# Weight blocks of a seven-product matrix multiplication: two sums made by an accumulating transfer, paired splits, and 15 instead of 12 of 22 tiles

## The chip, the cores and the metric

One core of one Trainium2 chip runs the whole program. The metric is the device time of one execution in microseconds, as the median of several runs. Engines are named as in the profile: PE (TensorE matmuls), PEld (its weight loads), DVE (VectorE), ACT (ScalarE), POOL (GpSimd), SP (SyncE, which here issues transfers).

## What is computed

Two layers, each of a feed-forward block, a mixer (an attention of several branches in the first layer, a latent attention "MLA" in the second) and a second feed-forward block, on 512 tokens of width 1024, all in 32-bit floats:

```
def _swiglu(x, w_gate, w_up, w_down):
    return (jax.nn.silu(x @ w_gate) * (x @ w_up)) @ w_down
...
for l in range(DEPTH):
    x = x + 0.5 * _swiglu(_rms_norm(x, ffn1_norm[l]), ffn1_w_gate[l], ffn1_w_up[l], ffn1_w_down[l])
    h = _rms_norm(x, mix_norm[l])
    ...
    x = x + 0.5 * _swiglu(_rms_norm(x, ffn2_norm[l]), ffn2_w_gate[l], ffn2_w_up[l], ffn2_w_down[l])
return _rms_norm(x, final_norm)
```

The feed-forward width is 2816, that is 22 tiles of 128. The change concerns the products with `w_gate` and `w_up` in the four feed-forward blocks.

## The kernel before, in words

The stages run in the order f0, e, f1, f2, m, f3: four feed-forward blocks (FFN) around the mixers e and m. Activations lie transposed, features on partitions and the 512 tokens along the free axis, as eight tiles of 128x512.

Every factor is split into a high part, rounded to the float32r format on ACT, and the remainder, made on DVE. A product is then three matmuls (`mm3`, lines 208 to 210): high by high, high by low, low by high.

An FFN (`ffn`) does its 22 tiles in two halves of 11, each followed by the down projection of that half. An ordinary tile takes the weights of gate and up, 128x1024 each; each product is 8 x 3 matmuls of 512 columns, 48 in all. A tile listed in `SEVEN` (line 32) treats gate and up together as a 2x2 block product: the two halves of the features by the two halves of the tokens. Seven products of half size (`seven`, lines 301 to 343) take the place of eight: 7 x 4 x 3 = 84 matmuls of 256 columns. Their left factors are four blocks of the weights and four sums: A11, A12, A22, r21 (which is only a summand), S1 = r21 + r22, S2 = S1 + A11, S3 = A11 + r21, S4 = A12 + S2. The right factors are halves of x and the tiles T12 and T34 that `combine` makes once in an FFN. Before the change the pattern of the tiles from 4 on is two with seven products, then one ordinary.

`fetch_seven` (line 164) makes the left factors: two loads of 512 KB on SP's queue (lines 170 and 171), four adds on DVE (line 174), and for each of seven blocks a copy on ACT (line 180) and a subtraction on DVE (line 181). They lie two by two in tiles `wh` and `wl`: (A11, S2), (S1, S3), (A12, S4), and A22 alone in `w3h` and `w3l`. For other weights `fetch` (line 144) loads 512 KB (line 154) and splits it in one piece of 1024 columns (lines 160 and 161).

What sets the order is a list of the weights in the order of use (`plan`) and `chunk`, which keeps two entries fetched ahead. Within that, a scheduler places each engine's instructions in one in-order queue; buffers (three each of `w`, `wh` and `wl`) decide how far a load or a split can really run ahead. On an engine's queue, whatever stands behind a waiting instruction waits with it.

Other lines that are spoken of: in `norm`, ACT and DVE split x (lines 217 and 218), `squares` adds squares on POOL (line 231), `rstd` sums them on PE (line 241) into `rv` (line 246, DVE) and takes the power on POOL (`rcol`, line 251), and `spread` turns that into the row `rrow` by four transposes on PE (line 260). The evacuation of a tile multiplies by this row.

Of the kernel before, what the change touches and what calls it, by code (L numbers as in the profile page):

```python
# [3 lines left out]
P = 128  # L4
D, SEQ, FF = 1024, 512, 2816
# [3 lines left out]
F32, F32R = mybir.dt.float32, mybir.dt.float32r  # L9
AF, OP, AX = mybir.ActivationFunctionType, mybir.AluOpType, mybir.AxisListType  # L10
# [14 lines left out]
def raw(ap):  # L25
    return ap.bitcast(F32)
# [2 lines left out]

SEVEN = (4, 5, 7, 8, 10, 11, 13, 14, 16, 17, 19, 20)

FFNS = {"f0": ("f1", 0, 0), "f1": ("f2", 0, 2), "f2": ("f1", 1, 3), "f3": ("f2", 1, 5)}

# [42 lines left out]
class Core:  # L78
# [47 lines left out]
    def plan(self, stages):  # L126

        todo = []
        for st in stages:
            if st in FFNS:  # L130
                name, l, _ = FFNS[st]
                for h in range(2):
                    for f in range(h * HF, h * HF + HF):
                        if f in SEVEN:
                            todo.append(("seven", name, l, f))
# [28 lines left out]
    def fetch_seven(self, name, l, f):  # L164

        nc, kp, sb = self.nc, self.keep, self.sb
        g, u = [kp.tile([P, 1024], F32, name="w", bufs=3) for _ in range(2)]
        nc.sync.dma_start(g, self.a[name + "_g"][l, f])  # L170
        nc.sync.dma_start(u, self.a[name + "_u"][l, f])
        a11, a12, r21, r22 = g[:, :SEQ], g[:, SEQ:], u[:, :SEQ], u[:, SEQ:]
        s1, s2, s3, s4 = [sb.tile([P, SEQ], F32, name=f"s{i}") for i in range(1, 5)]
        add = lambda o, a, b: nc.vector.tensor_tensor(o, a, b, OP.add)
        out = {}

        def parts(blocks, h, l):
            for i, (n, src) in enumerate(blocks):
                c = slice(i * SEQ, i * SEQ + SEQ)
                nc.scalar.activation(h[:, c], src, AF.Copy)  # L180
                nc.vector.tensor_tensor(l[:, c], src, raw(h[:, c]), OP.subtract)
                out[n] = h[:, c], l[:, c]

        def pair():
            return [kp.tile([P, 1024], F32R, name=n, bufs=3) for n in ("wh", "wl")]
        add(s1, r21, r22)
        add(s2, s1, a11)
        parts((("A11", a11), ("S2", s2)), *pair())
        add(s3, a11, r21)
        parts((("S1", s1), ("S3", s3)), *pair())  # L190
        add(s4, a12, s2)
        parts((("A12", a12), ("S4", s4)), *pair())
        parts((("A22", r22),), *[sb.tile([P, SEQ], F32R, name=n) for n in ("w3h", "w3l")])
        return out

    def chunk(self, *key):
# [148 lines left out]
    def ffn(self, name, l, gi, then=None):  # L345

        nc = self.nc
        with self.tc.tile_pool(name="ff", bufs=1, reuse_waits="tile") as sb:
# [3 lines left out]
            for half in range(2):  # L352
                ah, al = [], []
                for i in range(HF):
                    f = half * HF + i
                    a = sb.tile([P, SEQ], F32, name="fa", bufs=2)
                    if f in SEVEN:
                        g, n = self.seven(sb, ("seven", name, l, f), xs, T, R)
# [574 lines left out]
def constants(np):  # L933

    c = {"ident": np.eye(P, dtype=np.float32)}
    p = np.arange(P)[:, None]
    j = np.arange(SEQ)[None, :]
    d = p + 384 - j
    big = np.float32(BIG)
    c["mcau"] = np.where(d >= 0, np.float32(0), big).astype(np.float32)  # L940
    n = ((d >= 0) & (d <= 128)).astype(int) + ((d >= 0) & (d % 4 == 0)) + ((d >= 0) & (d % 16 == 0))
    c["mdil"] = np.where(n > 0, -np.log(np.maximum(n, 1).astype(np.float64)), BIG).astype(np.float32)
    t = np.arange(P)[:, None, None] + P * np.arange(4)[None, :, None]
    e = (16 * np.arange(32) + 31)[None, None, :]
    ok = (e <= t)
    c["mcmp"] = np.stack([np.where(ok, np.float32(0), big), ok.astype(np.float32)], axis=1).astype(np.float32)

    def table(dims):
        inv = np.float32(500000.0) ** (-np.arange(0, dims, 2, dtype=np.float32) / np.float32(dims))
        ang = np.arange(SEQ, dtype=np.float32)[:, None] * inv[None, :]  # L950
        return np.cos(ang).T, np.sin(ang).T
    co, si = table(16)
    cp, sp = np.ones((P, SEQ), np.float32), np.zeros((P, SEQ), np.float32)
    for b in (0, 64):
        cp[b:b + 8], cp[b + 8:b + 16] = co, co
        sp[b:b + 8], sp[b + 8:b + 16] = -si, si
    c["cos_p"], c["sin_p"] = cp, sp
    co, si = table(32)
    sc = np.float32(-(96.0 ** -0.5))
    one, c2, s2 = np.ones((64, SEQ), np.float32), np.concatenate([co, co]), np.concatenate([-si, si])  # L960
    c["cs_q"] = np.stack([np.concatenate([one, c2, s2]), np.concatenate([c2, s2, one])]) * sc
    c["cs_k"] = np.stack([np.tile(c2, (4, 1)), np.tile(s2, (4, 1))], axis=1)
    return {k: np.ascontiguousarray(v, dtype=np.float32) for k, v in c.items()}


def layout(np, i):

    i = {k: np.asarray(v) for k, v in i.items()}
    d = {"x": i["x"][0].T}
    d["g"] = np.concatenate(  # L970
        [v.reshape(-1, P).T for v in (i["ffn1_norm"][0], i["mix_norm"][0], i["ffn2_norm"][0], i["ffn1_norm"][1],
                                      i["mix_norm"][1], i["ffn2_norm"][1], i["final_norm"],
                                      i["mla_q_norm"][0], i["mla_kv_norm"][0])]
        + [np.zeros((P, 1), np.float32)], axis=1)
    for n in ("1", "2"):
        for s, t in (("gate", "g"), ("up", "u")):
            w = i[f"ffn{n}_w_{s}"]
            d[f"f{n}_{t}"] = w.reshape(2, KT, P, NF, P).transpose(0, 3, 2, 1, 4).reshape(2, NF, P, 1024)
        w = i[f"ffn{n}_w_down"].reshape(2, 2, HF, P, KT, P).transpose(0, 1, 4, 2, 3, 5)
        d[f"f{n}_d"] = w.reshape(2, 2, HF, 8, P, P).transpose(0, 1, 2, 4, 3, 5).reshape(2, 2, HF, P, 1024)  # L980

    def feat(w):

        k, n = w.shape[0] // P, w.shape[1] // P
        return w.reshape(k, P, n, P).transpose(2, 1, 0, 3).reshape(n, P, k * P)

    def out_parts(w, parts):

        w = w.reshape(8, P, KT, P)
        res = []  # L990
        for pairs in parts:
            n = len(pairs)
            v = w[list(pairs)].transpose(2, 0, 1, 3).reshape(n, 8, P, P)
            res.append(v.transpose(0, 2, 1, 3).reshape(n, P, 1024))
        return np.concatenate(res)

    def tok(w, n):

        w = w.reshape(KT, P, -1)
        pad = -KT % n  # L1000
        if pad:
            w = np.concatenate([w, np.zeros((pad,) + w.shape[1:], w.dtype)])
        return w.reshape(-1, n, P, w.shape[2]).transpose(0, 2, 1, 3).reshape(len(w) // n, P, -1)
    w = i["ev_w_in"][0]
    cols = [w[:, c:c + n] for c, n in ((C_QA, 512), (C_KC, 128), (C_VC, 128), (C_KS, 128), (C_KW, 128),
                                       (C_QB, 512), (C_KB, 512))]
    d["ev_in"] = feat(np.concatenate(cols, axis=1))
    d["ev_vsw"] = tok(np.concatenate([w[:, C_VS:C_VS + 128], w[:, C_VW:C_VW + 128], w[:, C_G:C_G + 24]], axis=1), 3)
    d["ev_vb"] = np.stack([tok(w[:, C_VB + 256 * j:C_VB + 256 * j + 256], 4) for j in range(2)])
    d["ev_out"] = out_parts(i["ev_w_out"][0], EV_PARTS)  # L1010
    w = np.stack([i[f"nsa_cmp_pos_{s}"][0].reshape(16, 2, 64).transpose(2, 1, 0) for s in "kv"], axis=1)
    d["pos"] = np.concatenate([w, w])
    d["cmp_w1"] = np.stack([i[f"nsa_cmp_{s}_w1"][0].reshape(2, 8, P, P).transpose(0, 2, 1, 3).reshape(2, P, 1024)
                            for s in "kv"])
    d["cmp_w2"] = np.stack([np.concatenate([i[f"nsa_cmp_{s}_w2"][0]] * 2, axis=1) for s in "kv"], axis=1)
    w = i["mla_w_in"][0]
    d["mla_in"] = feat(np.concatenate([w[:, :384]] + [w[:, 384:416]] * 4, axis=1))
    w = i["mla_w_uq"][0].reshape(2, P, 16, 96)
    n, r, z = w[..., :64], w[..., 64:], np.concatenate([w[..., 80:], w[..., 64:80]], axis=-1)
    w = np.stack([np.concatenate([n, r, z], axis=-1)[:, :, 0::2], np.concatenate([r, z, n], axis=-1)[:, :, 1::2]],  # L1020
                 axis=3)
    d["mla_uq"] = w.reshape(2, P, 4, 4, P).transpose(2, 1, 3, 0, 4).reshape(4, P, 1024)
    w = i["mla_w_ukv"][0].reshape(P, 2, 8, 2, 64).transpose(1, 0, 3, 2, 4)
    d["mla_ukv"] = w.reshape(2, P, 1024)
    d["mla_out"] = out_parts(i["mla_w_out"][0], ML_PARTS)
    d.update(constants(np))
    return {k: np.ascontiguousarray(v) for k, v in d.items()}
# [18 lines left out]
```

## Time and profile before

| | us |
|---|---|
| median of 3 runs | 1916.21 (1915.01 to 1916.22) |
| the profiled execution | 1913.86 |
| its span, first to last instruction | 1911.7 |
| PE busy | 1883.0 (98%) |
| DVE busy | 1354.5 (71%) |
| ACT busy | 903.4 (47%) |
| POOL busy | 274.6 (14%) |
| mean share of the DMA engines | 0.30, at 91 GB/s |

Matmuls overlap in the profile (each lasts longer than the distance to the next), so what a matmul costs is read from the distance between starts. The rows of the timeline give start, duration, engine, line, operation, result and operands, shape, and how many equal ones were merged; the windows give busy time by engine in a stretch of the span.

### The profile page before, as it was taken

Reading aid. Unit: us, or ns where it says so; the run is one execution under the profiler, and the core shown is the slowest. Engines: PE = TensorE matmul, PEld = TensorE weight load, DVE = VectorE, ACT = ScalarE, POOL = GpSimd, SP = SyncE. Lnnn points to the kernel's source line nnn. Section 1 sums busy time; section 2 is a strip of 40 time slices with the busy share of each in tenths; the row PEclk is TensorE's granted clock in tenths of the full one; section 3 lists DMA queues with packets and bytes.
Section 4 is the critical chain, followed back from the end, with each engine's and each line's share of the span. In section 5 each row is a group of like instructions: output and inputs, shape, how many; then the busy total and the mean of one; then the engine's idle time right before and its main releaser. Section 6 shows DMA issues by size and latency. Waiting matters only on the chain. (4 is left out here: it accounts for less than half of the span.)

```text
span 1911.7 us, 27981 instructions
## 1 busy us (share of the span) xinstructions
PE 1883.0 (98%) x10850; PEld 1657.4 (87%) x10850; DVE 1354.5 (71%) x2438; ACT 903.4 (47%) x1585; POOL 274.6 (14%) x291
## 2 busy tenths in 40 slices
PE   9999999999999999999999999999999999999998
PEld 6998998878887789889988988998878879989987
DVE  8764875477888888468756864885489888747853
ACT  7432443347586654234435432443378664424432
POOL 0000000274454400000010000000156320000001
PEclk9999999999999999999999999999999999999999
DMA  4232333323111123323333232333311122333231
GB/s 170 86 113 87 110 98 109 118 89 93 58 45 34 45 85 114 100 89 109 111 92 96 82 118 89 100 108 102 123 39 33 56 89 89 111 99 100 89 110 67
DMA packets 49846, 174.67 MB, mean 91 GB/s; under 512 B 5793, under 2 KB 6049, under 8 KB 49713
## 3 DMA queue, kind: packets, MB, share of 16 engines
q1 hardware_dynamic: 48960, 171.74, 29.1%
q8 instruction: 85, 1.39, 0.3%
q10 hardware_dynamic: 720, 1.08, 0.2%
q14 instruction: 49, 0.39, 0.1%
q0 software_dynamic: 32, 0.07, 0.0%
HBM read 170.76 MB, written 2.10 MB: 90 GB/s over the span
## 5 line engine op out<-in xcount | busy, mean ns | idle before, releaser
L160 ACT ACTIVATE wh<-w 128x1024 fp32r<-128x1024 f32 (+1 forms) x217 | 229.2, 1057 | 357.7 <-PE pt L209 98.3
L161 DVE TENSOR_TENSOR wl<-w,wh 128x1024 fp32r<-128x1024 f32 (+1 forms) x217 | 273.0, 1259 | 159.4 <-ACT wh L160 158.3
L208 PE MATMUL pa<-xh,wh 128*128 128x512 f32 (+1 forms) x736 | 269.1, 366 | 2.8 <-ACT wh L160 2.2
L210 PE MATMUL pa<-xh,wl 128*128 128x512 f32 (+1 forms) x736 | 268.2, 364 | 0.5 <-DVE wl L161 0.5
L209 PE MATMUL pa<-xl,wh 128*128 128x512 f32 (+1 forms) x736 | 268.7, 365 | 0.0
L231 POOL TENSOR_TENSOR of<-of,t 128x512 f32<-128x512 f32 x36 | 55.9, 1552 | 1319.6 <-issue 892.5
L209 PE MATMUL pb<-xl,wh 128*128 128x256 f32 (+1 forms) x704 | 233.9, 332 | 0.2
L208 PE MATMUL pb<-xh,wh 128*128 128x256 f32 (+1 forms) x704 | 233.6, 332 | 0.0
L210 PE MATMUL pb<-xh,wl 128*128 128x256 f32 (+1 forms) x704 | 233.3, 331 | 0.0
L180 ACT ACTIVATE wh<-w 128x512 fp32r<-128x512 f32 x96 | 60.7, 632 | 237.9 <-PE pb L209 159.2
L208 PEld LDWEIGHTS pa<-xh,wh 128*128 128x128 f32 x736 | 139.9, 190 | 26.0 <-ACT wh L160 3.5
L210 PEld LDWEIGHTS pa<-xh,wl 128*128 128x128 f32 x736 | 139.7, 190 | 22.1 <-DVE wl L161 1.0
L209 PEld LDWEIGHTS pa<-xl,wh 128*128 128x128 f32 x736 | 139.9, 190 | 20.8 <-DVE xl L218 0.4
L209 PEld LDWEIGHTS pb<-xl,wh 128*128 128x128 f32 x704 | 133.8, 190 | 15.0 <-DVE xl L218 2.6
L208 PEld LDWEIGHTS pb<-xh,wh 128*128 128x128 f32 x704 | 133.8, 190 | 12.9 <-ACT xh L217 0.4
L210 PEld LDWEIGHTS pb<-xh,wl 128*128 128x128 f32 x704 | 133.8, 190 | 12.3
L180 ACT ACTIVATE wh<-s 128x512 fp32r<-128x512 f32 x192 | 114.9, 622 | 55.9 <-PE pa L209 26.3
L208 PE MATMUL pc<-fah,wh 128*128 128x512 f32 x352 | 137.0, 389 | 0.0
L209 PE MATMUL pc<-fal,wh 128*128 128x512 f32 x352 | 137.0, 389 | 0.0
L210 PE MATMUL pt<-fah,wl 128*128 128x512 f32 x352 | 136.9, 389 | 0.0
L210 PE MATMUL pc<-fah,wl 128*128 128x512 f32 x352 | 136.9, 389 | 0.0
L208 PE MATMUL pt<-fah,wh 128*128 128x512 f32 x352 | 136.9, 389 | 0.0
(264 smaller groups left out, 4556.3 us busy)
## 6 DMA issues: line engine op xcount, KB each, us to landing
w<-f_g SPq DMA_DIRECT2D x88, 512.0 KB, 3.7
w<-f_u SPq DMA_DIRECT2D x88, 512.0 KB, 3.6
w<-f_d SPq DMA_DIRECT2D x88, 512.0 KB, 3.7
w<-ev_in SPq DMA_DIRECT2D x16, 512.0 KB, 3.7
w<-ev_out SPq DMA_DIRECT2D x8, 512.0 KB, 3.3
w<-mla_out SPq DMA_DIRECT2D x8, 512.0 KB, 3.3
x<-x SPq DMA_DIRECT2D x8, 256.0 KB, 5.3
w<-ev_vb SPq DMA_DIRECT2D x4, 512.0 KB, 3.2
```

The source lines that it names most:

```text
L160: nc.scalar.activation(h[:, :cols], w[:, :cols], AF.Copy)
L161: nc.vector.tensor_tensor(l[:, :cols], w[:, :cols], raw(h[:, :cols]), OP.subtract)
L180: nc.scalar.activation(h[:, c], src, AF.Copy)
L208: nc.tensor.matmul(out, wh, xh, start=start, stop=False)
L209: nc.tensor.matmul(out, wh, xl, start=False, stop=False)
L210: nc.tensor.matmul(out, wl, xh, start=False, stop=stop)
L231: eng.tensor_tensor(parts[0], parts[0], sq, OP.add)
```

## The change

`SEVEN` lists 15 tiles: from tile 4 on four with seven products follow each other, then one is ordinary (shorter at the end of a half: 9 and 10, 11 and 12, 19 to 21). The host lays the four blocks of such a tile out side by side as A12, r22, A11, r21 in one array `f1_s` or `f2_s`. S1 and S3 are no longer added on DVE: SP loads r21 twice side by side into a new tile `s13` (two buffers), and when it has landed POOL issues a transfer of r22 and A11, side by side, that adds to what lies there. A11 and A12 are loaded into the first halves of two `w` tiles, whose second halves take S2 and S4 from DVE. So each pair lies in one tile, and is split by one ACT copy and one DVE subtraction of 1024 columns. r22 has a tile of its own, with one buffer.

```
-SEVEN = (4, 5, 7, 8, 10, 11, 13, 14, 16, 17, 19, 20)
+SEVEN = (4, 5, 6, 7, 9, 10, 11, 12, 14, 15, 16, 17, 19, 20, 21)
...
-        g, u = [kp.tile([P, 1024], F32, name="w", bufs=3) for _ in range(2)]
-        nc.sync.dma_start(g, self.a[name + "_g"][l, f])
-        nc.sync.dma_start(u, self.a[name + "_u"][l, f])
-        a11, a12, r21, r22 = g[:, :SEQ], g[:, SEQ:], u[:, :SEQ], u[:, SEQ:]
-        s1, s2, s3, s4 = [sb.tile([P, SEQ], F32, name=f"s{i}") for i in range(1, 5)]
-        add = lambda o, a, b: nc.vector.tensor_tensor(o, a, b, OP.add)
+        src = self.a[name + "_s"][l, SEVEN.index(f)]
+        u1, u3 = [kp.tile([P, 1024], F32, name="w", bufs=3) for _ in range(2)]
+        u2 = sb.tile([P, 1024], F32, name="s13", bufs=2)
+        r22 = sb.tile([P, SEQ], F32, name="r22")
+        nc.sync.dma_start(u2.rearrange("p (a b) -> p a b", a=2),
+                          src[:, 3 * SEQ:].unsqueeze(1).to_broadcast([P, 2, SEQ]))
+        nc.gpsimd.dma_start(u2, src[:, SEQ:3 * SEQ], accum_op=OP.add)
+        nc.sync.dma_start(u1[:, :SEQ], src[:, 2 * SEQ:3 * SEQ])
+        nc.sync.dma_start(u3[:, :SEQ], src[:, :SEQ])
+        nc.sync.dma_start(r22, src[:, SEQ:2 * SEQ])
         out = {}
 
-        def parts(blocks, h, l):
-            for i, (n, src) in enumerate(blocks):
+        def parts(names, t, h, l):
+            nc.scalar.activation(h, t, AF.Copy)
+            nc.vector.tensor_tensor(l, t, raw(h), OP.subtract)
+            for i, n in enumerate(names):
                 c = slice(i * SEQ, i * SEQ + SEQ)
-                nc.scalar.activation(h[:, c], src, AF.Copy)
-                nc.vector.tensor_tensor(l[:, c], src, raw(h[:, c]), OP.subtract)
                 out[n] = h[:, c], l[:, c]
...
-        add(s1, r21, r22)
-        add(s2, s1, a11)
-        parts((("A11", a11), ("S2", s2)), *pair())
-        add(s3, a11, r21)
-        parts((("S1", s1), ("S3", s3)), *pair())
-        add(s4, a12, s2)
-        parts((("A12", a12), ("S4", s4)), *pair())
-        parts((("A22", r22),), *[sb.tile([P, SEQ], F32R, name=n) for n in ("w3h", "w3l")])
+        nc.vector.tensor_tensor(u1[:, SEQ:], u2[:, :SEQ], u1[:, :SEQ], OP.add)
+        parts(("A11", "S2"), u1, *pair())
+        parts(("S1", "S3"), u2, *pair())
+        nc.vector.tensor_tensor(u3[:, SEQ:], u3[:, :SEQ], u1[:, SEQ:], OP.add)
+        parts(("A12", "S4"), u3, *pair())
+        parts(("A22",), r22, *[sb.tile([P, SEQ], F32R, name=n) for n in ("w3h", "w3l")])
```

The first place is DVE's queue in the second half of f0, where the left factors of a seven-product tile are made between the evacuations of earlier tiles (numbers are buffer numbers). Before, for tile 14:

```order
L174 TENSOR_TENSOR s1_1938<-w_1935 128x512
L174 TENSOR_TENSOR s3_1940<-w_1934,w_1935 128x512
L174 TENSOR_TENSOR s2_1939<-s1_1938,w_1934 128x512
L373 TENSOR_TENSOR fa_1874<-pb_1968,fg_1993 128x512
L181 TENSOR_TENSOR wl_1900<-w_1875,wh_1899 128x512
L181 TENSOR_TENSOR wl_1900<-s4_1882,wh_1899 128x512
L377 TENSOR_TENSOR fal_1998<-fa_1874,fah_1997 128x512
L174 TENSOR_TENSOR s4_1941<-w_1934,s2_1939 128x512
L181 TENSOR_TENSOR wl_1945<-w_1934,wh_1944 128x512
L181 TENSOR_TENSOR wl_1945<-s2_1939,wh_1944 128x512
L330 TENSOR_TENSOR fv_2013<-fm_2014,pa_2008 128x256
L181 TENSOR_TENSOR wl_1952<-s1_1938,wh_1951 128x512
```

And now, around tiles 14 to 16 (`s13_2030`, `s13_2082` and `s13_2143` are the pairs S1, S3 of these three tiles; line 190 is the S2 add, 193 the S4 add, 183 the split):

```order
L183 TENSOR_TENSOR wl_2043<-s13_2030,wh_2042 128x1024
L379 TENSOR_TENSOR fal_2024<-fa_1915,fah_2023 128x512
L375 TENSOR_TENSOR fa_2027<-pb_2107,fg_2132 128x512
L183 TENSOR_TENSOR wl_2048<-w_2029,wh_2047 128x1024
L379 TENSOR_TENSOR fal_2137<-fa_2027,fah_2136 128x512
L190 TENSOR_TENSOR w_2141<-s13_2143,w_2141 128x512
L183 TENSOR_TENSOR wl_2091<-w_2080,wh_2090 128x1024
L332 TENSOR_TENSOR fv_2173<-fm_2174,pa_2168 128x256
L183 TENSOR_TENSOR wl_2095<-s13_2082,wh_2094 128x1024
L335 TENSOR_TENSOR fm_2174<-fv_2173,pt_2170 128x512
L193 TENSOR_TENSOR w_2142<-w_2142,w_2141 128x512
```

Four adds and pairs of small splits have become two adds and large splits. The S2 add of tile 16, which reads what the accumulating transfer left, stands ahead of the first split of tile 15 and of tile 14's evacuation.

The second place is SP's queue for the same tiles. Before, for tiles 13 and 14 (seven products) and the ordinary tile 15:

```order
L170 DMA w_1875<-f1_g 128x1024
L171 DMA w_1876<-f1_u 128x1024
L170 DMA w_1934<-f1_g 128x1024
L171 DMA w_1935<-f1_u 128x1024
L154 DMA w_2002<-f1_g 128x1024
L154 DMA w_2114<-f1_u 128x1024
```

And now, from the loads of A11 and A12 of tile 15 (`w_2080`, `w_2081`) to those of tile 17:

```order
L176 DMA w_2080<-f1_s 128x512
L177 DMA w_2081<-f1_s 128x512
L178 DMA r22_2083<-f1_s 128x512
L173 DMA s13_2143<-f1_s 128x2x512
L176 DMA w_2141<-f1_s 128x512
L177 DMA w_2142<-f1_s 128x512
L173 DMA s13_2276<-f1_s 128x2x512
L176 DMA w_2274<-f1_s 128x512
L178 DMA r22_2144<-f1_s 128x512
L177 DMA w_2275<-f1_s 128x512
```

The load of r21 for a pair of sums (line 173) stands ahead of the same tile's other loads, behind loads of the tile before that wait for their own buffers.

The third place is POOL's queue where f1 begins, after the last subtraction of the mixer e. Before, up to the same place of f2:

```order
L623 TENSOR_TENSOR ol<-of,oh 128x512
L231 TENSOR_TENSOR of<-of,t 128x512 x6
L251 TENSOR_TENSOR rcol<-rv,mhalf 128x4
L231 TENSOR_TENSOR of<-of,t 128x512 x6
L251 TENSOR_TENSOR rcol<-rv,mhalf 128x4
```

And now (line 175 is the accumulating transfer):

```order
L625 TENSOR_TENSOR ol<-of,oh 128x512
L233 TENSOR_TENSOR of<-of,t 128x512 x6
L175 DMA s_7047<-f_s 128x1024
L175 DMA s_7099<-f_s 128x1024
L253 TENSOR_TENSOR rcol<-rv,mhalf 128x4
```

The transfers of the first two seven-product tiles have come between the adds of squares and the power; the other 13 of the FFN follow behind it.

## Rows read from the trace of the kernel before

**Rows 1.** The page, part 1: busy time, share of the span, instructions.

```profile
PE 1883.0 (98%) x10850; PEld 1657.4 (87%) x10850; DVE 1354.5 (71%) x2438; ACT 903.4 (47%) x1585; POOL 274.6 (14%) x291
```

**Rows 2.** Timeline of PE, f0: first matmuls of tile 5, of 6, of 7.

```profile
66.35 0.28 PE L208 MATMUL pa<-xh,wh 128*128 128x256 f32 x1
...
76.43 0.40 PE L208 MATMUL pa<-xh,wh 128*128 128x512 f32 x1
...
87.34 0.28 PE L208 MATMUL pa<-xh,wh 128*128 128x256 f32 x1
```

**Rows 3.** Windows of these two tiles: busy by engine, PE clock, DMA share, GB/s.

```profile
66.35:76.43 10.08, 10.08 (x86) 10.08 (x85) 7.95 (x14) 4.92 (x7) 0.00 (x0) 1.00 0.53 158
76.43:87.34 10.91, 10.91 (x50) 9.02 (x49) 9.97 (x17) 4.18 (x7) 0.00 (x0) 1.00 0.31 96
```

**Rows 4.** The page, part 5: a group of instructions, idle before it, releaser.

```profile
L208 PE MATMUL pa<-xh,wh 128*128 128x512 f32 (+1 forms) x736 | 269.1, 366 | 2.8 <-ACT wh L160 2.2
```

**Rows 5.** Timeline of DVE back to back, f0: operations of 256, 512, 1024 columns.

```profile
40.28 0.75 DVE L295 TENSOR_TENSOR t<-t 128x256 f32<-128x256 f32 x2
40.95 0.68 DVE L371 TENSOR_TENSOR fg<-pa,rrow 128x512 f32<-128x512 f32 x1
41.55 0.68 DVE L298 TENSOR_TENSOR T12l<-t,T12h 128x512 fp32r<-128x512 f32 x1
42.15 1.29 DVE L174 TENSOR_TENSOR s<-w 128x512 f32<-128x512 f32 x2
43.35 1.22 DVE L161 TENSOR_TENSOR wl<-w,wh 128x1024 fp32r<-128x1024 f32 x1
44.49 0.69 DVE L181 TENSOR_TENSOR w3l<-w,w3h 128x512 fp32r<-128x512 f32 x1
```

**Rows 6.** Timeline of ACT back to back, f1.

```profile
674.64 1.04 ACT L160 ACTIVATE wh<-w 128x1024 fp32r<-128x1024 f32 x1
675.59 0.61 ACT L297 ACTIVATE T12h<-t 128x512 fp32r<-128x512 f32 x1
```

**Rows 7.** Transfers by issue: count, KB each, median us from issue to landing.

```profile
w<-f_g SPq DMA_DIRECT2D x88, 512.0 KB, 3.7
...
ident<-ident POOLq DMA_DIRECT2D x1, 64.0 KB, 3.8
```

**Rows 8.** DMA queues: packets, MB, share of 16 engines' span.

```profile
q1 hardware_dynamic: 48960, 171.74, 29.1%
```

**Rows 9.** Waits of DVE: us in total, times, longest.

```profile
DVE s L174 <- DMA w<-f_u: 17.1, 5, 3.8
```

**Rows 10.** Timelines of POOL, SP and PE where f1 begins, and two single issues.

```profile
662.31 3.87 POOL L231 TENSOR_TENSOR of<-of,t 128x512 f32<-128x512 f32 x2
671.59 1.14 POOL L251 TENSOR_TENSOR rcol<-rv,mhalf 128x4 f32<-128x4 f32 x1 [5.41 <-DVE rv L246]
...
653.47 0.33 SPq L154 DMA_DIRECT2D w<-f_g  x1
...
676.53 0.60 PE L260 MATMUL pt<-ident,rcol 128*128 128x128 f32 x4
...
1.23 0.76 POOL L108 DMA_DIRECT2D ident<-ident  x1 [0.79 <-POOLq L1038]
...
1529.71 0.33 SPq L154 DMA_DIRECT2D w<-f_g  x1
```

**Rows 11.** Timelines of POOL and DVE where f3 begins.

```profile
1543.69 5.05 POOL L231 TENSOR_TENSOR of<-of,t 128x512 f32<-128x512 f32 x3 [9.35 <-ACT t L229]
...
1543.45 0.74 DVE L218 SCALAR_TENSOR_TENSOR xl<-x,g,xh 128x512 fp32r<-128x512 f32 x1
...
1544.71 1.18 DVE L218 SCALAR_TENSOR_TENSOR xl<-x,g,xh 128x512 fp32r<-128x512 f32 x1
```

**Rows 12.** Window in the stage m, columns as in rows 3.

```profile
1390.00:1440.00 50.00, 45.10 (x254) 39.04 (x253) 45.66 (x121) 37.81 (x91) 27.99 (x33) 0.93 0.13 43
```

More of the change, by code (lines that the diff above doesn't have):

```diff
@@ L978, in layout @@
             d[f"f{n}_{t}"] = w.reshape(2, KT, P, NF, P).transpose(0, 3, 2, 1, 4).reshape(2, NF, P, 1024)
+        g, u = d[f"f{n}_g"][:, list(SEVEN)], d[f"f{n}_u"][:, list(SEVEN)]
+        d[f"f{n}_s"] = np.concatenate([g[..., SEQ:], u[..., SEQ:], g[..., :SEQ], u[..., :SEQ]], axis=-1)
         w = i[f"ffn{n}_w_down"].reshape(2, 2, HF, P, KT, P).transpose(0, 1, 4, 2, 3, 5)
```

## The prediction

> **What bounds the kernel now.** I read the shares of busy time first, then the timeline of TensorE (PE) alone, then the windows by stretch, and last the groups with their idle time. PE is busy 98% of the span [rows 1]. Its timeline shows a tile as the distance between first matmuls: a seven-product tile starts at 66.35, the next tile (an ordinary one) at 76.43, the next at 87.34 us [rows 2]. So one tile costs 10.08 us with seven products and 10.91 us without: 84 matmuls of 256 columns every 0.120 us against 48 of 512 columns every 0.227 us. In both stretches PE is busy all the time at granted clock 1.00, the higher level of 2.4 GHz, while DVE and ACT have room [rows 3]. In the whole run the FFN's products into `pa` waited 2.8 us for anything [rows 4]. The four FFNs are bound by PE alone, so whatever the change takes from DVE and ACT is worth nothing by itself; what counts is the number of seven-product tiles, and whether their weights still come in time.
>
> **The change, part by part.**
>
> *Three more seven-product tiles.* `SEVEN` grows from 12 to 15 of 22 tiles, in four FFNs: 12 ordinary tiles become seven-product ones. Each saves 10.91 - 10.08 = 0.83 us of PE [rows 2]: **10.0 us**, all of it on the path.
>
> *DVE per seven-product tile.* Back to back, DVE starts a 512-column operation every 0.60 us, a 1024-column one every 1.14, a 256-column one every 0.34 [rows 5]. Before, a tile took 4 adds and 7 splits of 512, and 4.0 us of evacuation (5 of 512, 3 of 256): 10.6 us, more than PE's 10.08. Now it takes 2 adds and a split of 512, and three splits of 1024: 5.2 + 4.0 = 9.2 us. Four such tiles in a row fit under PE's 40.3 us. Without that saving they would run 0.5 us behind in each tile. ACT starts a 1024-column copy every 0.95 us [rows 6]: and one of 512 takes 0.61: three of the one and four of the other are under 6 us. Both edits cost nothing, covered by PE.
>
> *Transfers.* A tile took two loads of 512 KB. Now it takes a load of r21 written twice (512 KB written), an accumulating transfer of 512 KB from POOL, and three loads of 256 KB. 1792 KB written in 10.08 us is 182 GB/s; the stretch of rows 3 had 158 GB/s at a DMA share of 0.53, so bandwidth is there.
>
> *When the sums land.* This is where the sum can fail, because the accumulation starts only when r21 has landed, and DVE's queue holds work behind the add that waits for it. A plain 512 KB load takes 3.7 us from issue to landing [rows 7]. For the accumulating one, call its time from POOL's issue to landing **A**; the trace has none. Below, A is 3.7: it moves at least the same bytes. Above: POOL's own 64 KB load took 3.8 us [rows 7], and the SP queue moved 171.74 MB in 29.1% of 16 engines' span [rows 8], which is 309 GB/s while busy, 1.7 us for 512 KB; were source, old sum and new sum three full passes, A = 3.8 + 3 x 1.7 = 8.9. I take one pass more than the plain load of the same size, its nearest row: **A = 5.4**. By the Trainium skill ("DMA: Bandwidth & Descriptors", section "Anatomy of one DMA — SWDGE (gpsimd) path") a POOL transfer takes about 2.0 us and its bytes at 436 GB/s: 3.2 us here, an estimate, 4.4 with a second pass; by it too the sum is the 10.0 us, with more room, but the trace's plain load is slower than that.
>
> Now follow the longest run, tiles 14 to 17, with t = 0 where PE starts tile 14 (in the queue listings, `s13_2143` is tile 16's pair of sums, `s13_2276` tile 17's). The pair for tile 16 can load when the split of tile 14's pair has freed its buffer, at -3.3 (PE frees that split's target in the middle of tile 13, at -5.5; copy 0.95, DVE 1.2 and what it does between). It lands at 0.5, the accumulation at 0.5 + A = 5.9. The add to S2 also needs A11, which waits for a `w` buffer until 2.2 and lands at 5.9. DVE waits in that add from 2.7 to 5.9, with the evacuation of tile 14 and the splits of tile 15 behind it. Then come the first pair of tile 15 at 7.7 (due 10.1), its second at 9.2 (due 13.0), the S4 add of tile 16 at 12.1 (its A12 is loaded only when the split at 7.7 frees a buffer, +3.7), the third pair of tile 15 at 14.2 (due 15.8). Tile 17's pair of sums loads from 9.3, lands at 13.0, is summed at 18.4; its S2 add ends at 19.0; the second pair of tile 16 is split at 21.1, due 23.0. Nothing is late on PE: DVE waits some 3 us in such an add, PE none. Waits of this kind exist already: DVE's adds waited 17.1 us for `w` in 5 places, up to 3.8 us, and PE did not feel it [rows 9]. The slack is 1.9 us behind two accumulations, so PE starts to wait at **A = 6.4**, 1.0 above my value. Cost taken: 0.
>
> *POOL at the start of an FFN.* Two accumulations now stand in POOL's queue between the adds of squares and `rcol`, for which PE's transposes wait. In f1 POOL is done with the adds at 666.2 and waits for `rv` until 671.59, and PE comes to the transposes at 676.53; SP issued the load ahead of the first sums at 653.47 [rows 10]. Both issues fit in that gap unless one takes over 4 us; POOL's load at the start kept it 0.76 [rows 10]. In f3 they stand ahead of the adds, which began at 1543.69 [rows 11]; the load ahead of theirs went out at 1529.71 [rows 10]. Cost 0.
>
> *POOL beside DVE.* DVE's split into `xl` took 0.74 us with POOL idle and 1.18 us with POOL adding from 1543.69 on [rows 11]: the two hinder each other. 60 issues of 0.76 us beside DVE would cost DVE some 26 us over the run if each slowed it like that, spread over 60 tiles that have 0.9 us each to spare: 0 on PE. The Trainium skill ("SBUF — State Buffer", section "SBUF: two separate sides") turns it round: while DVE holds the port pair that it shares with GpSimd, in a two-port mode, POOL can't write the descriptors of its transfers and they sit idle. It adds elsewhere that `tensor_tensor` has no such mode, and DVE's work in the FFN is nearly all of that kind; so I give it a small chance, below.
>
> *The MLA stage.* The scheduler wrote the queues anew there; in the first mixer they are the same. PE idles 4.9 us in the stretch that has most of this stage's gaps [rows 12]. A new order could lose as much again or win it all: +-5 us, taken as 0.
>
> **Sum.** 12 x 0.83 = 10.0 us. The profiled execution took 1913.86 us around its span of 1911.7 us, so 1903.9 on its own terms; the median of the runs is 2.35 above that execution: 1916.2 - 10.0 = **1906.2 us**.
>
> **Rivals.**
> 1. *The sums come too late* (slower). In the same table with A = 8: the S2 add of tile 16 ends at 9.1, tile 15's first pair is 0.2 us late, its third 0.7, and tile 16's second 2.3: PE loses 3.2 us in a run of four and 0.9 in the run of three. Two runs of four and one of three per FFN: 7.3 x 4 = 29 us, 1935 in all. With A = 7 it is 1.1 x 8 = 9 us, 1915. So from A = 7.1 on the kernel is slower than before, by some 20 us for each us more. For it: the reads of the old sums are of unknown price. Against it: A = 7.1 is twice a whole plain load. Chance 0.24 for over 7.1, 0.08 for between 6.4 and 7.1 (1906 to 1916).
> 2. *POOL's issues are starved by DVE* (slower). If an issue advanced only in the 0.9 us that DVE leaves free in a tile, A would grow by up to a tile's length, to 15 us; the loop of one buffer (3.7 + 15 + about 4 for add and splits) then exceeds two tiles (20.2), and by rival 1's slope the time is far above 1950. For it, rows 11; against it, that there both engines went on, 0.44 us slower and not stopped. Chance 0.04. This is where the port rule of the Trainium skill's page "SBUF — State Buffer" would lead.
> 3. *The MLA order decides* (either side): 1901 to 1911 with the tiles' gain, hence still faster; only with both at their bad ends no change. Chance 0.04.
>
> The forecast has 0.60.
>
> **How the numbers follow.** Forecast's own range: 1906.2 with the MLA's 5 us on either side, 1902 to 1911. With rival 1 up to A = 8 the range is **1902 to 1936**; left out are A above 8 and rival 2 (some 0.17) and a tail below. Changes under 0.2% (3.8 us) can hardly be told from none. Faster: the forecast, most of rival 3 and the lower half of A from 6.4 to 7.1, 0.67. Within 0.2%: the rest around A = 7.1, 0.08. Slower: 0.25.
>
> **What would show it.** Right: PE's timeline has 60 tiles of 10.08 us; PE's groups in the FFN have next to no idle time; POOL's transfers land in 4 to 6.4 us; DVE waits some us in the S2 adds for a DMA. Wrong: gaps of 1 to 3 us on PE ahead of the second pair of a run's third tile (16, 6), ended by the split of `s13`, with POOL's transfers over 6.4 us; or POOL issues of several us and `rcol` late at a stage's start.

## The result, and the profile after

| | us, median | runs from | ratio to before, 95% interval | profiled execution, its span |
|---|---|---|---|---|
| before | 1916.2 | 1915.0 to 1916.7 | | 1913.9, 1911.7 |
| changed | 1980.4 | 1973.0 to 1986.2 | 1.0334 [1.0296, 1.0371] | 1973.0, 1971.2 |

The change makes the kernel 64 us slower, where 10 us less were forecast. The profiled execution of the changed kernel is its fastest, so what its trace shows of the loss is the lower end. The first part of the page, which answers to [rows 1]:

```profile
PE 1895.6 (96%) x11282; PEld 1683.1 (85%) x11282; DVE 1349.7 (68%) x2306; ACT 909.0 (46%) x1477; POOL 323.8 (16%) x351
```

PE's share fell from 98% to 96% of a longer span: it waits more. For what, the view of PE's waits says (engine, tile and line that waited, what ended it, us in total, times, longest):

```profile
PE pt L212 <- DVE wl L183: 22.1, 7, 3.7
PE pb L212 <- DVE wl L183: 12.9, 12, 2.7
PE pa L212 <- DVE wl L183: 9.5, 10, 2.3
```

None of these three rows stands in the view of the kernel before. 29 times PE stood before a product with a low part that DVE had not yet split; measured from one matmul's start to the next, this is 50 us in all (a row's idle time is some 0.16 us less each time, because a matmul's modelled end lies behind the start of the next). DVE was at work in 41 of the 45 us of idle time that these rows add up to. It was working off what had piled up behind a wait of its own just before, mostly at line 190, the S2 add; in place of [rows 9], 17.1 us, its waits are:

```profile
DVE w L190 <- DMA s<-f_s: 102.5, 19, 6.9
DVE w L193 <- DMA w<-f_s: 54.5, 37, 3.4
DVE w L190 <- DMA w<-f_s: 35.1, 25, 3.0
```

19 times, up to 6.9 us, it waited for the accumulating transfer. The same run of tiles as in the prediction, 14 to 17 in f0, in the timelines of the four engines (start, duration, line, operation; in brackets the idle time before it). SP and POOL, the loads of r21 and the transfers that add to them:

```profile
223.83 0.38 SPq L173 DMA_DIRECT2D s<-f_s  x1
...
237.72 0.38 SPq L173 DMA_DIRECT2D s<-f_s  x1
...
228.39 0.87 POOL L175 DMA_DIRECT2D s<-f_s  x1 [19.31 <-DVE fal L379]
243.28 0.86 POOL L175 DMA_DIRECT2D s<-f_s  x1 [14.02 <-DVE fg L341]
```

DVE, with the S2 adds of tiles 16 and 17 and what stands behind each:

```profile
220.78 0.69 DVE L193 TENSOR_TENSOR w<-w 128x512 f32<-128x512 f32 x1 [0.72 <-DMA w<-f_s]
221.39 0.68 DVE L362 SCALAR_TENSOR_TENSOR fa<-fn,fg 128x512 f32<-128x512 f32 x1
221.99 0.68 DVE L373 TENSOR_TENSOR fg<-pa,rrow 128x512 f32<-128x512 f32 x1
222.59 1.21 DVE L183 TENSOR_TENSOR wl<-s,wh 128x1024 fp32r<-128x1024 f32 x1
...
234.40 0.69 DVE L190 TENSOR_TENSOR w<-s,w 128x512 f32<-128x512 f32 x1 [6.08 <-DMA s<-f_s]
235.01 1.22 DVE L183 TENSOR_TENSOR wl<-w,wh 128x1024 fp32r<-128x1024 f32 x1
...
236.47 1.22 DVE L183 TENSOR_TENSOR wl<-s,wh 128x1024 fp32r<-128x1024 f32 x1
...
250.18 0.69 DVE L190 TENSOR_TENSOR w<-s,w 128x512 f32<-128x512 f32 x1 [4.03 <-DMA s<-f_s]
...
251.72 1.22 DVE L183 TENSOR_TENSOR wl<-s,wh 128x1024 fp32r<-128x1024 f32 x1
```

PE, the first matmul of tile 14 and the three waits:

```profile
225.38 0.28 PE L210 MATMUL pa<-xh,wh 128*128 128x256 f32 x1
...
236.28 0.39 PE L212 MATMUL pa<-xh,wl 128*128 128x256 f32 x1 [0.43 <-DVE wl L183]
...
241.80 0.39 PE L212 MATMUL pb<-xh,wl 128*128 128x256 f32 x1 [0.92 <-DVE wl L183]
...
252.99 0.38 PE L212 MATMUL pt<-T12h,wl 128*128 128x256 f32 x1 [3.39 <-DVE wl L183]
```

Read downward: DVE stands still for 6.08 us ahead of the add at 234.40, and the split of tile 15's first pair, whose blocks have long been there, starts behind it at 235.01, so PE waits 0.43 us. Tile 17's load could go out only at 237.72, when the pair that held its buffer had been split; its sum is there at 250.18, and the second pair of tile 16, behind that add, makes PE wait 3.39 us. The whole kernel shows this pattern: in f0 the runs 4 to 7, 14 to 17 and 19 to 21 lose 4.6, 5.2 and 2.7 us from start to start; 9 to 12, which the down products break after tile 10, loses nothing.

The transfers, by issue (count, KB, median us from issue to landing; [rows 7] has 3.7 and 3.8). The last two are SP's plain loads for ordinary tiles; the kernel before has 3.7 and 3.6 for its loads of `f_g` and `f_u`:

```profile
s<-f_s SPq DMA_DIRECT2D x60, 512.0 KB, 4.3
s<-f_s POOLq DMA_DIRECT2D x60, 512.0 KB, 6.6
w<-f_s SPq DMA_DIRECT2D x120, 256.0 KB, 2.9
w<-f_g SPq DMA_DIRECT2D x28, 512.0 KB, 4.3
w<-f_u SPq DMA_DIRECT2D x28, 512.0 KB, 5.3
```

Windows of the changed kernel (columns as in [rows 3]): 3.0 of the 3.25 us for which PE waits in tile 6's S1 product in f0, the 3.4 us soon after, the next 3.4 us, and the stage m from its first `kh` product to f3's first product that waits for `x`:

```profile
80.60:83.60 3.00, 0.03 (x1) 0.03 (x1) 2.84 (x5) 0.63 (x1) 0.00 (x0) 1.00 0.02 9
84.00:87.40 3.40, 3.40 (x18) 3.40 (x17) 3.40 (x7) 0.17 (x1) 0.00 (x0) 0.50 0.73 177
87.40:90.80 3.40, 3.40 (x31) 3.40 (x30) 2.69 (x4) 1.79 (x3) 0.86 (x1) 1.00 0.79 222
...
1441.69:1591.43 149.74, 143.80 (x793) 123.24 (x793) 126.46 (x328) 107.37 (x253) 68.43 (x89) 0.98 0.19 56
```

DVE is busy for 2.84 of the 3.00 us of the first window, with what stood behind its wait. Two more losses are seen here. After the stall the granted clock is 0.50, the lower level of 1.2 GHz, for 3.4 us: 18 matmuls instead of 31. Between the start-up and the end, the trace before has 10.2 us at this level, that after 37.5 us; at half speed the 27 us more cost at most some 14 (PE was not busy in all of them). And the stage m, between the same two matmuls, took less before:

```profile
1396.93:1542.33 145.40, 141.49 (x794) 123.15 (x794) 124.97 (x327) 106.95 (x252) 70.09 (x87) 0.98 0.14 44
```

145.40 us against 149.74, 4.3 us more. So the two spans, 59.5 us apart, add up: -10.0 (12 tiles) + 50 (waits) + 14 (clock, at most) + 4.3 (stage m) = 58.

### The profile page after: what moved, and what is told of

The parts are those of the page before. It is cut to its first block, busy times and chain, and to the rows that moved or that the text cites. A ratio compares the mean times of both kernels' runs of the same rounds, so it can differ in the third digit from the quotient of the medians.

```text
span 1971.2 us, 29126 instructions
## 1 busy us (share of the span) xinstructions
PE 1895.6 (96%) x11282; PEld 1683.1 (85%) x11282; DVE 1349.7 (68%) x2306; ACT 909.0 (46%) x1477; POOL 323.8 (16%) x351
## 3 DMA queue, kind: packets, MB, share of 16 engines
q0 software_dynamic: 8672, 31.53, 9.6%
## 5 line engine op out<-in xcount | busy, mean ns | idle before, releaser
L160 ACT ACTIVATE wh<-w 128x1024 fp32r<-128x1024 f32 x193 | 203.8, 1056 | 307.7 <-PE pc L211 93.8
L161 DVE TENSOR_TENSOR wl<-w,wh 128x1024 fp32r<-128x1024 f32 x193 | 244.2, 1266 | 100.8 <-ACT wh L160 100.0
L212 PE MATMUL pa<-xh,wl 128*128 128x512 f32 (+1 forms) x688 | 245.9, 357 | 10.2 <-DVE wl L183 9.5
L210 PE MATMUL pa<-xh,wh 128*128 128x512 f32 (+1 forms) x688 | 245.5, 357 | 3.4 <-ACT wh L160 2.0
L211 PE MATMUL pa<-xl,wh 128*128 128x512 f32 (+1 forms) x688 | 244.6, 356 | 0.0
L212 PE MATMUL pb<-xh,wl 128*128 128x256 f32 (+1 forms) x704 | 225.2, 320 | 12.9 <-DVE wl L183 12.9
L211 PE MATMUL pb<-xl,wh 128*128 128x256 f32 (+1 forms) x704 | 224.0, 318 | 0.2
L210 PE MATMUL pb<-xh,wh 128*128 128x256 f32 (+1 forms) x704 | 224.0, 318 | 0.0
L175 POOL DMA_DIRECT2D s<-f_s x60 | 52.3, 876 | 1033.9 <-DMA s<-f_s 276.0
L182 ACT ACTIVATE wh<-w 128x1024 fp32r<-128x1024 f32 x120 | 126.5, 1054 | 150.0 <-PE pb L211 68.8
L183 DVE TENSOR_TENSOR wl<-w,wh 128x1024 fp32r<-128x1024 f32 x120 | 146.4, 1220 | 29.7 <-ACT wh L182 29.7
L210 PEld LDWEIGHTS pa<-xh,wh 128*128 128x128 f32 x688 | 131.0, 191 | 23.5 <-ACT wh L160 3.4
L211 PEld LDWEIGHTS pa<-xl,wh 128*128 128x128 f32 x688 | 131.0, 190 | 17.2 <-DVE xl L220 0.4
```

Of the source, the lines that this page charges most:

```text
L160: nc.scalar.activation(h[:, :cols], w[:, :cols], AF.Copy)
L161: nc.vector.tensor_tensor(l[:, :cols], w[:, :cols], raw(h[:, :cols]), OP.subtract)
L175: nc.gpsimd.dma_start(u2, src[:, SEQ:3 * SEQ], accum_op=OP.add)
L182: nc.scalar.activation(h, t, AF.Copy)
L183: nc.vector.tensor_tensor(l, t, raw(h), OP.subtract)
L210: nc.tensor.matmul(out, wh, xh, start=start, stop=False)
```

## The experiments

The theory after the trace (T1): the sums come too late in runs of three tiles or more, because load and accumulation stand one behind the other and can start only when a buffer of s13 comes free, and DVE, waiting in the S2 add, holds back splits of an earlier tile. Rivals: DVE is too slow for runs of four whatever the transfers do; POOL's issues are held up beside DVE; the DMA engines are full. Each kernel was timed beside the kernel before on the same chip.

| run | tiles | us, median | ratio to before, interval |
|---|---|---|---|
| e1 three buffers of s13 | 15 | 1913.8 | 0.9993 [0.9984, 1.0002] |
| e2 sums on DVE, one buffer of r21, r22 | 15 | 1940.5 | 1.0120 [1.0098, 1.0141] |
| e3 the change with runs of two | 12 | 1915.5 | 1.0002 [0.9993, 1.0011] |
| e4 the old fetch | 15 | 1910.3 | 0.9974 [0.9965, 0.9984] |
| e5 plain instead of accumulating transfer | 15 | 1931.6 | 1.0086 [1.0072, 1.0099] |
| e6 sums on DVE, two buffers | 15 | 1909.0 | 0.9970 [0.9958, 0.9983] |
| e7 three buffers of s13 | 18 | 1956.7 | 1.0214 [1.0183, 1.0244] |
| e8 the old fetch | 18 | 1906.4 | 0.9958 [0.9945, 0.9970] |
| e9 11 buffers of fah and fal | 15 | 1978.7 | 1.0336 [1.0312, 1.0360] |
| e10 S2 add on POOL | 15 | 1924.4 | 1.0051 [1.0036, 1.0067] |
| e11 as e6 | 18 | 1917.5 | 1.0012 [1.0003, 1.0021] |
| e12 e1 and e10 together | 15 | 1913.9 | 0.9994 [0.9985, 1.0003] |

**e1: a third buffer for the sums.**

```diff
-        u2 = sb.tile([P, 1024], F32, name="s13", bufs=2)
+        u2 = sb.tile([P, 1024], F32, name="s13", bufs=3)
-                    h = sb.tile([P, SEQ], F32R, name="fah", bufs=HF + 1)
-                    lo = sb.tile([P, SEQ], F32R, name="fal", bufs=HF + 1)
+                    h = sb.tile([P, SEQ], F32R, name="fah", bufs=HF)
+                    lo = sb.tile([P, SEQ], F32R, name="fal", bufs=HF)
```

> The changed kernel with three buffers for the pair (S1, S3) instead of two (paid for by one buffer fewer of each of the tiles fah and fal). The load of r21 then need not wait for the split of the pair two tiles earlier. Late sums (the chain load of r21, accumulation, S2 add, split, next load): the gaps on TensorE in runs of three and four tiles (some 53 us in all) go, and with them most of the 15 us at the lower clock: 1906 to 1925 us, DVE's wait for a DMA in the S2 adds well under 50 us instead of 102.5. DVE too slow for runs of four (whatever the transfers do): no change, 1975 to 1985. POOL's issues starved beside DVE, or the DMA engines full: no change or little, 1965 to 1985.

1913.8 us: one buffer gives 67 us back. Of PE's three rows of waits this is left, and the transfers are no faster (PE's waits, then the transfers by issue):

```profile
PE pb L212 <- DVE wl L183: 0.8, 2, 0.6
PE pt L212 <- DVE wl L183: 0.5, 1, 0.5
```
```profile
s<-f_s SPq DMA_DIRECT2D x60, 512.0 KB, 4.6
s<-f_s POOLq DMA_DIRECT2D x60, 512.0 KB, 7.2
```

The accumulating transfer even takes 7.2 us instead of 6.6, and nobody waits for it: DVE's row of waits at line 190 for `s` is gone. In one point the expectation failed: DVE still waits 73.1 us for a DMA in the S2 adds, not well under 50. These waits are for A11 (35.1 us in the changed kernel), and PE does not feel them. Neither a full DMA nor POOL nor DVE's speed can have been the cause. T1 stands; what counts is when the chain may start.

**e9: what e1 paid with, alone.** The two lower lines of e1's edit and no third buffer.

> The changed kernel with one buffer fewer of fah and fal (11 instead of 12 each) and nothing else: what e1 and e6 paid with. PE is done with the first half's activations some 10 us before the second half writes its first, so this should do nothing: 1973 to 1987 as the changed kernel. If the smaller tiles by themselves change the order for the better, part of e1's gain is theirs: under 1960.

1978.7, as the changed kernel. So e1's gain, and that of e6 and e12, which pay in the same way, is that of the buffers they bought.

**e3: the change with the 12 tiles of before.**

```diff
-SEVEN = (4, 5, 6, 7, 9, 10, 11, 12, 14, 15, 16, 17, 19, 20, 21)
+SEVEN = (4, 5, 7, 8, 10, 11, 13, 14, 16, 17, 19, 20)
```

> The changed kernel's way of fetching (accumulating transfer, paired splits) with the 12 tiles of the kernel before, in runs of two. Late sums that are carried from tile to tile of a run (the third tile's load waits for the first one's split): no run has a third tile, so no gap: 1914 to 1922 us. If a single accumulation is already too slow by itself, or the issues on POOL are: 48 tiles with a gap of some 0.5 to 1.0 us each, 1940 to 1965. DVE too slow for long runs: 1914 to 1920.

1915.5, no different from before, with 48 accumulating transfers at the same 6.6 us. A late sum alone is hidden; it takes a third tile, whose load waits for the first one's split.

**e4: the kernel before with 15 tiles.** Only `SEVEN` of the kernel before is replaced by that of the change.

> The kernel before with nothing changed but the list of tiles: 15 instead of 12, in runs of up to four. DVE needs 10.6 us per tile against PE's 10.08. Late sums as the cause: 0.5 us behind per tile, 2 us at the end of a run of four, within the lead of two fetched tiles: 1904 to 1925 us. DVE too slow for runs of four: 1960 to 1990, the loss of the changed kernel or more.

1910.3, faster than before, with no wait for a split on PE in the FFNs. DVE's 10.6 us per tile against PE's 10.08 do no harm in runs of four: the rival that DVE is too slow falls, and so does the need for the changed way of fetching at this number of tiles.

**e2 and e6: the sums on DVE, the pairs split at once.**

```diff
-        u2 = sb.tile([P, 1024], F32, name="s13", bufs=2)
-        nc.sync.dma_start(u2.rearrange("p (a b) -> p a b", a=2),
-                          src[:, 3 * SEQ:].unsqueeze(1).to_broadcast([P, 2, SEQ]))
-        nc.gpsimd.dma_start(u2, src[:, SEQ:3 * SEQ], accum_op=OP.add)
+        u2 = sb.tile([P, 1024], F32, name="s13")
+        r21 = sb.tile([P, SEQ], F32, name="r21")
+        nc.sync.dma_start(r21, src[:, 3 * SEQ:])
...
+        nc.vector.tensor_tensor(u2[:, :SEQ], r21, r22, OP.add)
...
+        nc.vector.tensor_tensor(u2[:, SEQ:], u1[:, :SEQ], r21, OP.add)
```

> The changed kernel without the accumulating transfer: S1 and S3 are added by DVE from loads of r21 and r22, the paired splits and the 15 tiles stay. DVE has 4 adds and a split of 512 and three splits of 1024: 5 x 0.60 + 3 x 1.14 + 4.0 = 10.4 us per tile against PE's 10.08. Late sums: the chain is gone, DVE falls 0.3 us behind per tile of a run, which the ordinary tile behind it gives back: 1903 to 1915 us. DVE too slow in runs of four: DVE has 1.2 us more per tile than in the changed kernel, so 1980 or more. POOL or its contention with DVE: as with late sums.

A miss: 1940.5, outside all that T1 allowed. The trace names the reason, a buffer that I had made scarce myself. The S1 add now needs r22, whose only buffer is freed by the last split of the tile before; its load comes late, and DVE waits for it in the S1 add (DVE's waits, then PE's):

```profile
DVE s L178 <- DMA r<-f_s: 35.5, 28, 2.8
```
```profile
PE pa L211 <- ACT wh L182: 10.6, 8, 2.6
```

e6 gives r21 and r22 two buffers each (paid for as in e1):

> As e2 (sums by DVE, paired splits, 15 tiles), but r21 and r22 with two buffers each (paid for as in e1). In e2 SP's queue waited 160 us for the add that freed r21's only buffer. If that buffer made e2 slow, and pairs split at once cost nothing: DVE has 10.4 us per tile against 10.6 in e4, so 1905 to 1912, no gaps in the FFNs. If splitting a pair at once is itself late (A11 waits for S2, both halves of the target must be free): 1925 to 1940 again, with gaps of 0.6 us or more ahead of the S1 product.

1909.0, without a wait for a split on PE; DVE's row above has shrunk from 28 waits to one of 0.9 us. SP's wait before the load of r21, which the expectation names, was not the sign of it: 160 us in e2, 171 us in e6, where PE feels nothing. To split pairs at once costs nothing; the difference between e2 and e6 (besides what e9 shows to be nothing) is again where a load may start.

**e5: the same transfers without the addition.**

```diff
-        nc.gpsimd.dma_start(u2, src[:, SEQ:3 * SEQ], accum_op=OP.add)
+        nc.gpsimd.dma_start(u2, src[:, SEQ:3 * SEQ])
```

> The changed kernel, but POOL's transfer writes its 512 KB instead of adding them (two buffers as in the change, same loads, same waits, same DVE work); left out: the addition of r21 in S1 and S3. Late sums, with the accumulation itself as the slow part: POOL's transfer falls from 6.6 to some 4 us, below the 6.4 from which the table makes PE wait: most of the 60 to 70 us come back, 1908 to 1930. Late sums, with the two transfers one behind the other and POOL's issue as the slow part: the transfer stays at 5.5 us or more and the time at 1950 to 1985. DMA engines full: 1960 to 1985.

1931.6, just above what was expected of a slow accumulation: 49 of the 64 us come back, not all. The transfers by issue, the queue's share of the 16 engines (for the changed kernel it is the row below this one), and PE's waits:

```profile
s<-f_s SPq DMA_DIRECT2D x60, 512.0 KB, 4.2
s<-f_s POOLq DMA_DIRECT2D x60, 512.0 KB, 5.0
...
q0 software_dynamic: 8672, 31.53, 5.0%
```
```profile
q0 software_dynamic: 8672, 31.53, 9.6%
```
```profile
PE pt L212 <- DVE wl L183: 9.0, 7, 1.9
PE pb L212 <- DVE wl L183: 3.9, 4, 1.4
PE pa L212 <- DVE wl L183: 1.5, 2, 1.1
```

A plain 512 KB from POOL takes 5.0 us, 1.6 less than the accumulating one. For the same 31.53 MB the accumulating packets keep the engines busy for 189 us (9.6% of 1971.2), the plain ones for 97 (5.0% of 1930.7): twice as long. The Trainium skill ("Collectives: The Full Stack", section "The bandwidth ceiling: the fold count and why AG ≠ RS ≠ AR") says of the addition in a ReduceScatter, a collective whose sums are made in the DMA transfers, that it is slower because it needs two source reads where a copy needs one, and gives it about half a copy's rate; the two shares, 9.6% and 5.0%, agree with that ratio. That the second read is the reason here too, no run shows.

**e10: the waiting add on another queue.**

```diff
-        nc.vector.tensor_tensor(u1[:, SEQ:], u2[:, :SEQ], u1[:, :SEQ], OP.add)
+        nc.gpsimd.tensor_tensor(u1[:, SEQ:], u2[:, :SEQ], u1[:, :SEQ], OP.add)
```

> The changed kernel with the S2 add (the one that waits for the accumulation) on POOL instead of DVE, two buffers as in the change. If the loss is that DVE, waiting 5 to 7 us in this add, holds back the splits of the tile before that stand behind it in its queue: the chain of transfers is as long as before, but only the tile itself waits for it, the gaps shrink and 1910 to 1940 comes out. If the chain from load to load is too long for the two buffers whoever waits in it: 1965 to 1995, and the adds on POOL take 1 us more.

1924.4: with two buffers and the accumulation left as they are (it even takes 7.0 us), 56 us come back when the waiting add leaves DVE's queue, though it takes 1.29 us on POOL instead of 0.69. A few other operations on DVE changed places with a neighbour. In its fastest run, the profiled one (1917.0), PE has 3.8 us of the 12.9 left at `pb`, and the wait stands on POOL, where none of the splits is behind it (PE's waits, then POOL's):

```profile
PE pb L212 <- DVE wl L183: 3.8, 3, 2.4
```
```profile
POOL w L190 <- DMA s<-f_s: 89.1, 15, 7.6
```

So the late sum itself costs little. Most of the loss is that DVE, in order, lets the splits of the tile before it wait as well.

**e12: both cures.** The edits of e1 and e10.

> The three buffers of e1 and the S2 add on POOL of e10 together, 15 tiles. If late sums and the blocked queue of DVE are the whole loss, no gap over 0.5 us is left in the FFNs and what is left of the forecast is its 10.0 us less the 4 us that the mixers' new order costs in e4: 1907 to 1911. If the adds on POOL slow DVE beside them, or the w buffers now end the waits: 1914 to 1925, as e1 or e10 alone.

1913.9, as e1 alone, not the 1907 to 1911 of a full cure. Its trace has one wait for a split left, 2.4 us in tile 9 of f1, and 17 us at the lower clock where e4 has 7. Some 4 us against e4 and e6 are not explained further.

**e7, e8, e11: 18 tiles.** `SEVEN = tuple(range(4, 22))` in e1, in the kernel before and in e6.

> As e1 (three buffers for the pair), with all tiles from 4 to 21 as seven-product ones, 18 of 22. DVE has 9.2 us per tile against PE's 10.08. Late sums cured by the third buffer: 12 more tiles x 0.83 = 10 us less than e1, 1901 to 1910. If three buffers only move the lateness to the fifth or sixth tile of a run: 1925 or more, with gaps from tile 8 and tile 15 on.

> The kernel before with 18 of 22 tiles (4 to 21), in runs of 7 and 11. DVE needs 10.6 us per tile against 10.08: 3.6 us behind at the end of a run of seven, 5.7 after eleven. If the lead of two fetched tiles covers that: 1898 to 1905. DVE too slow for long runs: stalls of 0.5 us a tile from about the fifth tile on and a lower clock behind them, 1910 to 1935.

> As e6 (sums by DVE, paired splits, two buffers of r21 and r22), with tiles 4 to 21. DVE has 10.4 us per tile against PE's 10.08; e8 has 10.6 and lost some 2 us in each second half. If DVE's time is the only limit: fewer and smaller gaps than e8, 1899 to 1905. If the pairs, split at once, or the three w buffers, of which a tile takes two until its third split, cost lead in long runs: 1907 to 1930.

e8, the kernel before with nothing changed but the list, is the fastest of all, 1906.4, faster than both kernels. It sits between its two expectations, and its limit shows in a window at the end of f0's run of eleven (columns as above):

```profile
262.40:284.50 22.10, 20.96 (x171) 20.35 (x169) 22.10 (x41) 11.62 (x22) 0.00 (x0) 1.00 0.34 109
```

DVE is busy for 22.10 of 22.10 us: here, at the end of the run of eleven, it is the bound (PE's waits for left factors of these tiles in f0 stand only there, 0.41 us at each). e7 shows the next scarce thing of the change when the sums are in time (its waits of PE, then of DVE):

```profile
PE pb L212 <- DVE wl L183: 20.2, 26, 2.0
PE pt L212 <- DVE wl L183: 16.9, 9, 3.0
```
```profile
DVE w L193 <- DMA w<-f_s: 83.3, 54, 3.4
DVE w L190 <- DMA w<-f_s: 71.1, 35, 6.3
```

DVE waits for A12 and A11 now, not for `s`: a tile holds one of the three `w` buffers until its first pair is split and another until its third, and in a run of eleven no ordinary tile gives the time back; this is read from the trace and not tested. e11 (1917.5) has less DVE work than e8 and is slower; it shares these `w` buffers, and SP stands before the loads of A11 and A12 for 182 and 185 us until a split frees one. That this decides in e11 was not tested by itself.

## Why the prediction was wrong

**The gain is there.** The 0.83 us per tile held: with the fetch out of the way, e4 and e6 came to 1910.3 and 1909.0, which is within 1.5 us of 10.0 less and the stage m's 4.3 more.

**The step that failed is "When the sums land".** The chain was right, link by link, and each link was too short. With t = 0 at 225.38, where PE starts tile 14:

| | forecast | measured |
|---|---|---|
| load of r21 for tile 16 issued | -3.3 | -1.55 |
| POOL's transfer issued | 0.5 | 3.0 |
| S2 add of tile 16 starts | 5.9 | 9.0 |
| first pair of tile 15 split, due 10.1 | 7.7 | 10.85 |
| load of r21 for tile 17 issued | 9.3 | 12.3 |
| POOL's transfer issued | 13.0 | 17.9 |
| S2 add of tile 17 starts | 18.4 | 24.8 |
| second pair of tile 16 split, due 23.0 | 21.1 | 27.6 |

Of the 3.1 us by which the first add is late, 1.75 are the start. The forecast's -3.3 is -5.5 with the copy and the split, and nothing for "what it does between". In the trace, ACT's copy of the pair starts 0.5 us behind an activation of tile 12, and the split stands on DVE behind an S4 add and two operations of evacuation, rows 220.78 to 221.99 above. ACT's rows:

```profile
220.09 0.63 ACT L361 ACTIVATE fg<-fg 128x512 f32<-128x512 f32 x1 [4.86 <-DVE fg L341]
220.63 1.05 ACT L182 ACTIVATE wh<-s 128x1024 fp32r<-128x1024 f32 x1
```

0.86 are the load, 4.56 us instead of 3.7. Only 0.6 are the accumulation, 6.0 instead of A = 5.4. For tile 17 the three are 3.0, 1.9 and 1.5, since each delay is handed on.

**A itself was mis-sized in its base, not in its pass.** I took a plain load of SP, 3.7, and 1.7 for one pass more. The pass is 1.6 (e5: 5.0 to 6.6); the base was POOL's own, 5.0. Part of that need not be POOL's: beside the new traffic SP's plain 512 KB loads for ordinary tiles also took longer, 4.3 and 5.3 us in the changed kernel and 4.1 and 4.7 in e5, against 3.7 and 3.6 before. How much is the queue and how much the traffic, no run separates. The estimate from the Trainium skill ("DMA: Bandwidth & Descriptors", section "Anatomy of one DMA — SWDGE (gpsimd) path"), 3.2 us or 4.4 with a second pass, was lower still than the 5.0 and 6.6 of the runs; the measurement decides.

**The break-even was true only for the other two links as forecast.** A = 6.4 supposed a load at -3.3 that takes 3.7. The start enters once and the load in both chains, 1.75 + 2 x 0.86 = 3.5 us, where tile 16's second pair had 1.9 us of room; A enters there twice, so by these numbers PE begins to wait at A = 5.4 - (3.5 - 1.9) / 2 = 4.6, an estimate. e5, with 5.0, agrees: its rows of PE's waits for a split add up to 14.4 us, and it is slower than before by 0.86%. What ran is nearly the row "A = 8" of rival 1: the S2 add of tile 16 ends at 9.1 forecast and 9.7 measured, waits of 0.2, 0.7 and 2.3 us against 0.43, 0.92 and 3.39. I had the bounds of A from 3.7 to 8.9 on the table, but gave the whole uncertainty to A and none to the load and the start, with a slack of 1.0 us for the three.

**Rival 1 was the right rival, and still too cheap.** 29 us of stalls were worked out at A = 8; 50 us of waits came, and up to some 14 us for the clock's fall behind them, which no term had. The slope was right without the clock: from start to start, e5's waits on PE are 33 us fewer than the changed kernel's for 1.6 us of A, 20 per us.

**The other points.** Four tiles in a row on DVE: no trouble, and, as e4 shows, none with the old 10.6 us either; the 0.5 us behind in each tile that the change was to save were covered anyway. DMA bandwidth: right (e1). POOL at the start of an FFN: right; the longest issue was 1.17 us. Rival 2: fell; the issues took 0.87 us with DVE beside them, 1.17 at most, so the lock that the Trainium skill ("SBUF — State Buffer", section "SBUF: two separate sides") describes for two-port modes made no difference here. POOL beside DVE: right; DVE's splits of 1024 columns took 1.22 us in the mean, as in [rows 5], beside the 60 issues. The MLA order, taken as 0 within 5 us: at its bad end, +4.3 us. e4 has the same 149.7 us with the old fetch, e3 with 12 tiles 145.1, e8 with 18 145.9: it is the order that the queues get there (PE's is the same in e4 as in the changed kernel, and the same in e3 as before), not the transfers.

## What to carry to other kernels

A chain that starts when a buffer comes free has to be summed from the operation that frees it, with all that stands ahead of that in its queue; its slack is compared with the doubt of all links together. A wait in an in-order queue costs what is queued behind it: a buffer more (67 us here) or a queue where nothing urgent stands behind (56 us) can be worth more than a faster transfer. And of a change with several parts, the cheapest alone should be tried first: the list of tiles alone gave 1910.3 us with the change's 15 tiles and 1906.4 us with 18, with none of the rest.

## What was not expected of the hardware

- An accumulating transfer of 512 KB into SBUF took 6.6 us (5.5 to 9.4) from POOL's issue, the same bytes written plainly 5.0; its issue held POOL for 0.87 us instead of 0.53, and its packets kept the DMA engines busy twice as long (9.6% against 5.0%).
- A plain 512 KB from POOL was slower than one from SP: 5.0 us against 3.7 in the kernel before and 3.6 to 4.7 for SP's loads of 512 KB in the FFNs of the same run.
- Six of PE's seven longest waits for a split (2.7 to 3.7 us) came with a stretch at granted clock 0.50, which began up to 1.3 us behind the wait's end, once within the wait; the wait of 3.39 us at 252.99 had none behind it. In the changed kernel these stretches added at most about a quarter to what the waits cost.
